# A hybrid transformer layer: its first norm as transposes, compression fed from PSUM, and another order of projections and attention

## The chip, the cores and the metric

The kernel runs on one core of a Trainium2 chip. A core has five engines that run side by side, each with its own queue of instructions in order: PE (TensorE: matmuls from SBUF into PSUM, which has 8 banks of 128 partitions by 512 fp32), DVE (VectorE), ACT (ScalarE), POOL (GpSimd, which sees SBUF only) and SP (SyncE, which issues DMAs). An instruction that waits holds up all that are behind it on its engine. The metric is the device time of one execution in microseconds: before the change 849.62 us, the median of 3 runs (848.8 to 850.38).

## The reference

One layer on x of 512 tokens by 1024, in fp32. Cut to what matters here:

```python
h = rms_norm(x, mix_norm_pre)
y = h @ w_in                      # q, kc vc, ksl vsl, kwn vwn, gates, mq mk mv, mi mf, mo
k_cmp = compress_blocks(kc, cmp_pos_k, w1_k, w2_k)   # blocks of 32 tokens, stride 16: 31 blocks
v_cmp = compress_blocks(vc, cmp_pos_v, w1_v, w2_v)   # silu((blocks + pos) @ w1) @ w2
o = gate0 * softmax(q k_cmp) v_cmp + gate1 * softmax(q ksl) vsl + gate2 * softmax(q kwn) vwn
mq, mk = silu(causal_depthwise_conv(mq, mk))         # width 4
y_ml = sigmoid(mo) * rms_norm(mlstm(mq, mk, mv, mi, mf))
x = x + rms_norm(concat(o, y_ml) @ w_out)
x = x + rms_norm(cross_attention(rms_norm(x), mem)); x = x + rms_norm(swiglu(rms_norm(x)))
```

There are 8 attention heads in 2 groups (kv 0 and 1) of width 64, and 4 mlstm heads. The 8 blocks of 64 tokens are all selected, so the selected branch is causal attention.

## The kernel before, in words

Matmuls of fp32 data run as three passes on a high and a low part (`split`: ACT makes `hi`, and VectorE or GpSimd makes `lo` = source - `hi`; `mm3` at L286 to L288: low x high, high x low, high x high). `H` holds the normed and turned x as such a pair, 1024 on partitions (8 k tiles) by 512 tokens.

**Head** (written out by hand, so its order on four engines is the order of the code). Rows of 128 tokens: `square_of` (ACT) sums squares, `gain_of` (VectorE, L480) multiplies x by the gain spread over partitions, `factor_of` takes the root (GpSimd) and makes a diagonal of it (L485), `turn_row` (L491) is eight fp32 matmuls of x by that diagonal, which the chip runs as 16, `parts_of` splits the result into `H` (`hTh`, `hTl`). `gates_and_v` is projection A of a row, 24 matmuls of 288 columns into `bk_A`: attention's values and all gates; its weights are split into `wah`, `wal` as they land. `bk_A` has PSUM tag "d" with two buffers; `keep_a` empties one: `vf`, `vr` and `gt_all`, `gl` (L512). Then come the mlstm's values `bk_mv`.

**Middle.** `PLAN["order"]` lists what is started in turn, and a scheduler with priorities orders the instructions on each engine by it. Lower-case names are projections, each name one tile: `c0`, `c1` convolution pairs, `m0`, `m2` the mlstm's output gate, `kc` the compression's input, `ks` keys, `q0` queries. Each tile splits 1024 x 128 weights (`whi`, `wlo`), runs 24 matmuls into `bk_dT` (tag "d") and has an evacuation: `ev_conv` (L709 to L716), `ev_mo` (L723, L724), `ev_kcvc`. The last adds the positions into `Xr` (L811, eight VectorE instructions of 64x248) and splits them into `Xb`. `Ck` and `Cv` are the compression's first matmul, 8 weight splits `w1s` and 16 matmuls into `bk_hb` (L880); each `Ck` in the list runs two of the eight. `S` and `O` are an mlstm head's scores (`bk_ms`, weighted into `sT`; L764 makes the weights from `rb`, a row fetched from DRAM to all partitions) and output (`bk_mn`, `hnat`, `ym`). `bk_ms`, `bk_hb` and attention's `bk_sc` and `bk_pc` share PSUM tag "sc" with three buffers.

**Attention.** `PLAN["units"]` lists 16 units (kv, row, pair of heads). Each runs `scores` (`bk_sc`, L977 to L981, `mx` is the minimum beside it) and then `values` of the unit before (transposes `bk_tr`, products `bk_pv`). `PLAN["fill"]` puts other work after a unit: `q` a query tile of kv 1, `C` the compressed branch of kv 0 (`compressed`: `bk_pc`, then on VectorE L682 to L695, and transposes `bk_pcT`), `m` and `k` of the memory. Then w_out, cross-attention and the feed-forward follow.

Of the kernel before, what the change touches and what calls it, by code (L numbers as in the profile page):

```python
# [86 lines left out]

# [1365 lines left out]
```

## Time and profile before

| | |
|---|---|
| median of 3 runs | 849.62 us (848.8 to 850.38) |
| the profiled execution | 849.66 us, of which its span is 847.9 |
| PE busy in the span | 821.3 us (97%) |
| DVE busy | 542.3 us (64%) |
| ACT busy | 425.1 us (50%) |
| POOL busy | 299.2 us (35%) |
| chain that ended last: PE | 78% |
| the same: DVE, ACT, POOL | 7%, 3%, 1% |

The profile is of one execution. Busy time is the time in which an engine ran an instruction, so TensorE's 821.3 us include those at a lower clock. The rows further down are from the trace of the same execution. "A <- B" in a list of waits says that A stood idle until B was done; a row's bracket at its end is the idle time before it. Times are us from the start of the span.

### The profile page before, as it was taken

The page shows a single profiled execution, that of the slowest core. Times are in us where ns is not written, and L with a number is a line of the kernel's source. Part 1 is how long each engine was busy: PE and PEld are TensorE (multiplying, and loading weights), DVE is VectorE, ACT ScalarE, POOL GpSimd, SP SyncE. Part 2 cuts the span into 40 slices and gives each one's busy share as a digit, 9 for nine tenths or more (in the row PEclk, how much of TensorE's full clock was granted, in tenths as well). Part 3 has the DMA queues.
Part 4 walks back from the last instruction along what each step waited for, and adds up shares of the span by engine and source line. Part 5 has one row for each costly group of instructions (what it writes and reads, how often), then busy time and mean ns, then how long its engine had stood idle before and what let it go on. Part 6 is the DMA issues. An engine that isn't in the chain of part 4 may idle for free.

```text
span 847.9 us, 12708 instructions
## 1 busy us (share of the span) xinstructions
PE 821.3 (97%) x4870; PEld 707.7 (83%) x4870; DVE 542.3 (64%) x934; ACT 425.1 (50%) x840; POOL 299.2 (35%) x224
## 2 busy tenths in 40 slices
PE   8999989999999999999999999999999999999997
PEld 5977767886688978778888889999999999888885
DVE  5738696697879835843453769988877885224323
ACT  5524565858867743743452556444444444324311
POOL 2043332355537542511320111444444444323320
PEclk9999999998999999999999999999999999999999
DMA  8371323221203232251341033333333322232102
GB/s 246 95 229 63 100 66 107 99 69 50 76 1 100 94 133 73 70 179 53 137 160 50 0 125 105 121 111 111 111 113 113 108 106 100 100 100 100 49 26 75
DMA packets 67763, 83.18 MB, mean 98 GB/s; under 512 B 4368, under 2 KB 53873, under 8 KB 67702
## 3 DMA queue, kind: packets, MB, share of 16 engines
q1 hardware_dynamic: 64574, 77.97, 28.3%
q10 hardware_dynamic: 3128, 4.40, 1.6%
q8 instruction: 38, 0.62, 0.3%
q14 instruction: 23, 0.19, 0.1%
HBM read 80.24 MB, written 2.12 MB: 97 GB/s over the span
## 4 chain that ended last, share of the span: by engine, by line
PE 78%; DVE 7%; ACT 3%; issue 1%; POOL 1%; DVEq 0%; ACTq 0%; POOLq 0%
PE bk_X L1301 5%; PE bk_X L1302 5%; PE bk_X L1303 5%; PE bk_ff L286 5%; PE bk_ff L288 5%; PE bk_ff L287 5%; PE bk_dT L286 4%; PE bk_dT L287 4%; PE bk_dT L288 4%; PE bk_pv L1027 3%; PE bk_dN L287 3%; PE bk_dN L286 3%; PE bk_dN L288 3%; PE bk_Z L1301 2%; PE bk_Z L1302 2%; PE bk_Z L1303 2%
## 5 line engine op out<-in xcount | busy, mean ns | idle before, releaser
L166 ACT ACTIVATE whi<-raw 128x1024 fp32r<-128x1024 f32 (+1 forms) x80 | 76.8, 968 | 63.4 <-PE bk_dT L286 27.8
L167 DVE TENSOR_TENSOR wlo<-raw,whi 128x1024 fp32r<-128x1024 f32 x41 | 54.2, 1323 | 81.5 <-PE bk_ff L287 43.0
L167 POOL TENSOR_TENSOR wlo<-raw,whi 128x1024 fp32r<-128x1024 f32 x23 | 55.8, 2428 | 106.4 <-ACT whi L166 104.6
L166 ACT ACTIVATE wh<-raw 128x1024 fp32r<-128x1024 f32 x64 | 67.3, 1057 | 49.3 <-PE bk_X L1301 16.1
L167 POOL TENSOR_TENSOR wl<-raw,wh 128x1024 fp32r<-128x1024 f32 x19 | 55.5, 2921 | 97.5 <-ACT wh L166 70.2
L286 PE MATMUL bk_dT<-hTh,wlo 128*128 128x512 f32 x192 | 76.9, 401 | 1.1 <-DVE wlo L167 0.8
L287 PE MATMUL bk_dT<-hTl,whi 128*128 128x512 f32 x192 | 76.3, 397 | 0.0
L288 PE MATMUL bk_dT<-hTh,whi 128*128 128x512 f32 x192 | 76.1, 396 | 0.0
L167 DVE TENSOR_TENSOR wl<-raw,wh 128x1024 fp32r<-128x1024 f32 x45 | 64.6, 1440 | 9.2 <-ACT wh L166 9.2
L167 POOL TENSOR_TENSOR gs<-gf,gs 128x512 fp32r<-128x512 f32 x22 | 32.4, 1478 | 65.9 <-ACT gs L166 65.9
L1302 PE MATMUL bk_X<-A,wh 128*128 128x256 f32 x192 | 54.5, 284 | 1.0 <-DVE A L167 1.0
L1301 PE MATMUL bk_X<-A,wl 128*128 128x256 f32 x192 | 54.4, 283 | 0.4 <-ACT A L166 0.4
L1303 PE MATMUL bk_X<-A,wh 128*128 128x256 f32 x192 | 54.3, 283 | 0.0
L287 PE MATMUL bk_ff<-wlo,gs 128*128 128x512 f32 x128 | 49.8, 389 | 0.0
L288 PE MATMUL bk_ff<-whi,gs 128*128 128x512 f32 x128 | 49.6, 389 | 0.0
L1301 PE MATMUL bk_X<-AS,wl 128*128 128x256 f32 x160 | 45.6, 285 | 2.4 <-ACT u L1356 2.3
L286 PE MATMUL bk_ff<-whi,gs 128*128 128x512 f32 x128 | 47.4, 389 | 0.0
L997 POOL TENSOR_SCALAR s<-s,acf 128x128 f32<-128x128 f32 (+3 forms) x32 | 36.5, 1151 | 26.7 <-PE bk_tr L1012 15.9
L1302 PE MATMUL bk_X<-AS,wh 128*128 128x256 f32 x160 | 44.9, 281 | 0.0
L1301 PE MATMUL bk_Z<-AS,wl 128*128 128x256 f32 x160 | 44.9, 281 | 0.0
L1303 PE MATMUL bk_X<-AS,wh 128*128 128x256 f32 x160 | 44.9, 281 | 0.0
L1303 PE MATMUL bk_Z<-AS,wh 128*128 128x256 f32 x160 | 44.9, 280 | 0.0
(376 smaller groups left out, 2535.2 us busy)
## 6 DMA issues: line engine op xcount, KB each, us to landing
raw<-in_w_gate_up_dram SPq DMA_DIRECT2D x22, 1024.0 KB, 6.5
raw<-in_w_down_dram SPq DMA_DIRECT2D x11, 1024.0 KB, 4.9
raw<-in_w_xkv_dram SPq DMA_DIRECT2D x8, 1024.0 KB, 5.1
raw<-in_w_in_dram SPq DMA_DIRECT2D x7, 1024.0 KB, 5.3
raw<-in_w_out_dram SPq DMA_DIRECT2D x4, 1024.0 KB, 5.1
raw<-in_w_xq_dram SPq DMA_DIRECT2D x4, 1024.0 KB, 5.4
raw<-in_w_xo_dram SPq DMA_DIRECT2D x4, 1024.0 KB, 5.1
raw<-in_w_in_dram SPq DMA_DIRECT2D x6, 512.0 KB, 4.7
```

Of the source, the lines that this page charges most:

```text
L166: first = nc.scalar.activation(hi, src, AF.Copy)
L167: second = (eng or nc.vector).tensor_tensor(lo, src, hi.bitcast(F32), op=OP.subtract)
L286: nc.tensor.matmul(o, lhsT=wl, rhs=xh, start=start, stop=False)
L287: nc.tensor.matmul(o, lhsT=wh, rhs=xl, start=False, stop=False)
L288: return nc.tensor.matmul(o, lhsT=wh, rhs=xh, start=False, stop=stop).ins
L997: ENG[on].tensor_scalar(s[:, 0:n], s[:, 0:n], c, None, op0=OP.mult)
L1027: nc.tensor.matmul(o, lhsT=v, rhs=pTs[br][q][:, j], start=(br, j, q) == mms[0], stop=(br, j, q) == mms[-1])
L1301: nc.tensor.matmul(o, lhsT=wl[:, k, c], rhs=A.hi(n, k), start=st, stop=False, skip_group_check=True)
L1302: nc.tensor.matmul(o, lhsT=wh[:, k, c], rhs=A.lo(n, k), start=False, stop=False, skip_group_check=True)
L1303: nc.tensor.matmul(o, lhsT=wh[:, k, c], rhs=A.hi(n, k), start=False, stop=stop and k == 3, skip_group_check=True)
```

## The change

The head makes the normed row on VectorE (`norm_half`: x times factor times gain) and turns it by transposes. Rows of x are fetched earlier, row 1's turn lies between the two halves of projection A of row 0, and `keep_a` of a row comes after the parts and the norm of later rows. The compression's input is copied to its hi part by ACT straight out of PSUM and the lo part is subtracted by VectorE (64x496 each); the positions go into a column (block 31) that no block uses, and `fold`, by which `bk_hb` is turned, adds that column to all blocks. The first step of the convolution and the output gate's scale go from VectorE to ACT. `rd` and `rb` go from ACT's DMA queue to SP's, `rb` two heads ahead. Half of v's weight splits come in halves, in other buffers. Two lists change.

```diff
-        "order": "c0 Lk c0 Lv kc m0 m0 Ck Ck Ck Ck c1 kc S0 O0 c1 "
-                 "S1 Cv Cv Cv Cv m2 S2 m2 O2 ks O1 ks q0 S3 q0 O3",
+        "order": "c0 Lk c0 Lv kc m0 Ck Ck m0 Ck Ck c1 kc S0 O0 c1 "
+                 "Cv S1 Cv m2 Cv S2 Cv m2 O2 ks O1 ks q0 S3 q0 O3",
-        "fill": ["C", "", "", "q", "q", "", "mk", "", "ck", "k", "kkk", "k", "k", "", "", ""],
+        "fill": ["q", "", "C", "q", "", "", "mk", "", "ck", "k", "kkk", "k", "k", "", "", ""],
-        "w1tv": "WWWWWWWW",
+        "w1tv": "GWGWGWGW",
...
-    def gain_of(i, g):
+    def factor_of(i):
+        factor[i] = rstd_of(factor[i], 1)
+
+    def norm_half(i, g):
         if g == 0:
-            xg[i] = x4([P, D], name="xg")
+            xn[i] = x4([P, D], name="xn")
         c = slice(512 * g, 512 * g + 512)
-        nc.vector.tensor_tensor(xg[i][:, c], res(i)[:, c], g_in[g], op=OP.mult)
-
-    def factor_of(i):
-        r = rstd_of(dg[i], 1)
-        dg[i] = small([P, P], "mt1")
-        nc.vector.tensor_scalar(dg[i], ident, r, None, op0=OP.mult)
+        nc.vector.scalar_tensor_tensor(xn[i][:, c], res(i)[:, c], factor[i], g_in[g], op0=OP.mult, op1=OP.mult)
...
-            nc.tensor.matmul(b[:, 128 * k:128 * k + 128], lhsT=xg[i][:, 128 * kk:128 * kk + 128], rhs=dg[i],
-                             start=True, stop=True)
+            nc.tensor.transpose(b[:, 128 * k:128 * k + 128], xn[i][:, 128 * kk:128 * kk + 128], ident)
...
             done = gates_and_v(i, 1)
-            last = (done, *keep_a(i - 1))
             if i + 2 < NT:
                 square_of(i + 2)
-                for g in range(2):
-                    gain_of(i + 2, g)
+                factor_of(i + 2)
             if then:
                 for g in range(2):
                     parts_of(i + 1, g)
+            if i + 2 < NT:
+                for g in range(2):
+                    norm_half(i + 2, g)
+            last = (done, *keep_a(i - 1))
...
-    nc.scalar.dma_start(rd, rr)
+    nc.sync.dma_start(rd, rr)
...
-            nc.vector.tensor_scalar(y, u, cw(c, 3), cb(c), op0=OP.mult, op1=OP.add)
+            nc.scalar.activation(y, b, AF.Identity, scale=cw(c, 3), bias=cb(c))
...
-            nc.vector.tensor_scalar(sg[c], sg[c], 1.0, hn(c), op0=OP.add, op1=OP.mult)
+            nc.scalar.activation(sg[c], sg[c], AF.Identity, scale=hn(c), bias=hn(c))
...
-                for q in range(2):
-                    nc.vector.tensor_tensor(Xr[q][64 * r:64 * r + 64, :, 32 * kv:32 * kv + 31],
-                                            full[:, r, :, q:q + 31],
-                                            pt[:, 8 * q:8 * q + 8].rearrange("p (j o) -> p j o", o=1).to_broadcast([64, 8, 31]),
-                                            op=OP.add)
...
-                split(B[:, :, 0, :], B[:, :, 1, :], X[:, 4 * g:4 * g + 4, :], engines("xb")[g])
...
+                full.append(bass.AP(tensor=one.tensor, offset=one.offset, ap=[one.ap[0], [16, 2], [2, 8], [16, 31]]))
+                to.append(X[64 * r:64 * r + 64, :, :, :, 32 * kv:32 * kv + 31])
+        for q in range(4):
+            nc.scalar.activation(to[q][:, :, :, 0], full[q], AF.Copy)
+        for q in range(4):
+            nc.vector.tensor_tensor(to[q][:, :, :, 1], full[q], to[q][:, :, :, 0].bitcast(F32), op=OP.subtract)
...
+    every = small([P, 1], "every", 1)
+    nc.vector.tensor_copy(every, fold[:, 31:32])
+    nc.vector.tensor_scalar(fold, fold, every, None, op0=OP.add)
```

The rows below are what stands in an engine's queue. VectorE in the head, from `hTl` of row 1 on, before (`vr` and `gl` are of `keep_a`; `xg` and `mt_275` the row times the gain and the diagonal):

```order
L167 TENSOR_TENSOR hTl<-bk_pn,hTh 128x4x128 x2
L232 TENSOR_SCALAR rs_e<-ss 128x1
L485 TENSOR_SCALAR mt_275<-cc,rs_r 128x128
L167 TENSOR_TENSOR vr<-bk_A,vr 128x2x64
L512 TENSOR_TENSOR gl<-bk_A,gb 128x8
L480 TENSOR_TENSOR xg<-xin,gain 128x512 x2
L167 TENSOR_TENSOR hTl<-bk_pn,hTh 128x4x128 x2
```

and now:

```order
L166 TENSOR_TENSOR hTl<-bk_pn,hTh 128x4x128 x2
L482 SCALAR_TENSOR_TENSOR xn<-xin,rs_r,gain 128x512 x2
L231 TENSOR_SCALAR rs_e<-ss 128x1
L166 TENSOR_TENSOR hTl<-bk_pn,hTh 128x4x128 x2
L482 SCALAR_TENSOR_TENSOR xn<-xin,rs_r,gain 128x512 x2
L166 TENSOR_TENSOR vr<-bk_A,vr 128x2x64
L508 TENSOR_TENSOR gl<-bk_A,gb 128x8
L166 TENSOR_TENSOR hTl<-bk_pn,hTh 128x4x128 x2
```

`vr` and `gl` of row 0 stood ahead of the gain step and the parts of row 2, and stand behind the parts of row 2 and the norm of row 3.

ACT around the first `Ck`, before (`qm`, `kmA` are of the mlstm's scores, `u` of the convolution):

```order
L709 ACTIVATE u<-bk_dT 128x512
L828 ACTIVATE qm<-zc 64x512
L715 ACTIVATE u<-zc 128x512
L166 ACTIVATE whi<-raw 128x1024
L824 ACTIVATE kmA<-zc 64x512 x2
L747 DMA rb<-rd 128x512
L166 ACTIVATE Xb<-Xr 128x4x64 x4
L764 ACTIVATE sT<-rb,ub 128x128 x3
```

and now:

```order
L715 ACTIVATE u<-bk_dT 128x512
L716 ACTIVATE zc<-bk_dT,chan 128x512
L831 ACTIVATE qm<-zc 64x512
L165 ACTIVATE w1s<-w_700 128x2x256
L721 ACTIVATE u<-zc 128x512
L821 ACTIVATE Xb<-bk_dT 64x16x31 x4
L165 ACTIVATE w1s<-w_702 128x2x256
L827 ACTIVATE kmA<-zc 64x512 x2
L165 ACTIVATE whi<-raw 128x1024
```

The convolution's first step has come in, the copies of `Xb` have nearly twice the elements per partition and come from `bk_dT`, and `whi` stands behind them.

VectorE at the first units of attention, before (`pc`, `mn`, `cf` are of the branch; `s,mx` of a unit's scores; `qst` of a query tile):

```order
L684 TENSOR_TENSOR pc<-pc,bk_pc 128x256
L687 TENSOR_REDUCE mn<-pc 128x16
L688 TENSOR_TENSOR pc<-pc,mn 128x512
L829 SCALAR_TENSOR_TENSOR qst<-bk_dT,qst 64x512
L691 TENSOR_REDUCE cf<-pc 128x16
L791 TENSOR_SCALAR hnat<-hnat,rs_r 128x128 x4
L829 SCALAR_TENSOR_TENSOR qst<-bk_dT,qst 64x512
L692 RECIPROCAL cf<-cf 128x16
L981 ISA s,mx<-bk_sc,nB 128x256
```

and now, some 20 instructions later in the queue:

```order
L690 TENSOR_TENSOR pc<-pc,bk_pc 128x256 x2
L693 TENSOR_REDUCE mn<-pc 128x16
L694 TENSOR_TENSOR pc<-pc,mn 128x512
L697 TENSOR_REDUCE cf<-pc 128x16
L698 RECIPROCAL cf<-cf 128x16
L699 TENSOR_TENSOR cf<-cf,gt_all 128x16
L700 TENSOR_SCALAR cf<-cf,cc 128x4
L701 TENSOR_TENSOR pc<-pc,cf 128x512
L993 ISA s,mx<-bk_sc,nB 128x128
```

The branch's steps stood between those of the last queries and of `hnat`; they stand in one piece, after `hnat` and the scores of the first units.

## Rows read from the trace of the kernel before

**Rows 1.** Windows: stretch; us, busy time per engine (instructions), clock, DMA share, GB/s.
```profile
10.00:36.00 26.00, 23.42 (x160) 21.27 (x159) 17.21 (x35) 14.53 (x38) 4.95 (x7) 1.00 0.39 127
80.00:110.00 30.00, 28.80 (x136) 22.74 (x136) 20.91 (x36) 15.80 (x34) 10.20 (x8) 1.00 0.41 113
110.00:130.00 20.00, 15.23 (x63) 10.79 (x62) 19.13 (x43) 15.78 (x42) 7.35 (x6) 0.91 0.08 20
180.00:200.00 20.00, 17.21 (x78) 13.22 (x76) 17.87 (x63) 11.77 (x29) 12.87 (x12) 0.83 0.20 59
```

**Rows 2.** The same view, two us inside the start of attention.
```profile
196.00:198.00 2.00, 2.00 (x9) 1.68 (x8) 1.68 (x6) 2.00 (x9) 1.57 (x2) 0.50 0.22 43
```

**Rows 3.** Waits of TensorE, 10 to 36 us: sum, times, longest.
```profile
PE bk_A L287 <- POOL wal L167: 1.4, 3, 0.8
PE bk_A L286 <- DVE hTl L167: 0.5, 1, 0.5
```

**Rows 4.** Waits of TensorE, 80 to 130 us.
```profile
PE bk_hb L880 <- DVE w1s L167: 2.9, 3, 1.6
PE bk_ms L756 <- DVE sT L766: 1.7, 1, 1.7
PE bk_dT L286 <- DVE wlo L167: 0.8, 2, 0.6
```

**Rows 5.** Waits of TensorE, 180 to 200 us.
```profile
PE bk_sc L977 <- DVE mx L981: 1.1, 1, 1.1
PE bk_mt L792 <- DVE hnat L791: 1.0, 1, 1.0
PE bk_pcT L698 <- DVE pc L695: 0.6, 1, 0.6
```

**Rows 6.** Timeline of TensorE, head: start, duration, instruction, count.
```profile
7.35 3.75 PE L491 MATMUL bk_pn<-mt,xg 128*128 128x128 f32 x16
...
18.46 1.95 PE L491 MATMUL bk_pn<-mt,xg 128*128 128x128 f32 x16
```

**Rows 7.** Timeline of TensorE, 227 to 230 us.
```profile
227.92 1.04 PE L254 MATMUL bk_pn<-cc,xn 128*128 128x128 f32 x8
```

**Rows 8.** Instructions of line 250: duration in ns, least, median, most.
```profile
L250 DVE SCALAR_TENSOR_TENSOR xn<-xin,rs_r,gain x12: 742/749/753, 335.6 to 497.3; 128x512 f32<-128x512 f32 x12
```

**Rows 9.** Timeline of VectorE, head.
```profile
13.19 1.89 DVE L480 TENSOR_TENSOR xg<-xin,gain 128x512 f32<-128x512 f32 x2
...
22.69 0.28 DVE L167 TENSOR_TENSOR vr<-bk_A,vr 128x128 fp32r<-128x128 f32 x1
23.23 0.17 DVE L512 TENSOR_TENSOR gl<-bk_A,gb 128x8 f32<-128x8 f32 x1 [0.26 <-ACT gt_all L511]
23.32 1.29 DVE L480 TENSOR_TENSOR xg<-xin,gain 128x512 f32<-128x512 f32 x2
24.76 0.69 DVE L167 TENSOR_TENSOR hTl<-bk_pn,hTh 128x512 fp32r<-128x512 f32 x1 [0.15 <-ACT hTh L166]
```

**Rows 10.** Groups of ACT, 60 to 150 us: count, busy us, mean ns, idle before.
```profile
L166 ACT ACTIVATE Xb<-Xr 128x256 fp32r<-128x256 f32 x8 | 2.7, 409 | 1.8 <-DVE Xr L811 1.8
...
L709 ACT ACTIVATE u<-bk_dT 128x512 f32<-128x512 f32 x4 | 2.3, 580 | 0.0
```

**Rows 11.** Windows, TensorE instructions of bk_dT alone, 97 to 103 us.
```profile
97.00:103.00 6.00, 6.00 (x28) 4.86 (x27) 0.00 (x0) 0.30 (x1) 1.00 0.60 177
```

**Rows 12.** Groups of VectorE, 80 to 130 us.
```profile
L811 DVE TENSOR_TENSOR Xr<-bk_dT,chan 64x248 f32<-64x248 f32 x16 | 6.0, 409 | 0.1
...
L710 DVE TENSOR_SCALAR zc<-u,chan 128x512 f32<-128x512 f32 x2 | 4.2, 2080 | 4.9 <-ACT u L709 4.9
L167 DVE TENSOR_TENSOR Xb<-Xr,Xb 128x256 fp32r<-128x256 f32 x8 | 4.0, 555 | 0.0
```

**Rows 13.** Groups of VectorE, 180 to 200 us.
```profile
L682 DVE TENSOR_TENSOR pc<-bk_pc,nB 128x7 f32<-128x7 f32 (+3 forms) x16 | 1.7, 166 | 0.0
...
L695 DVE TENSOR_TENSOR pc<-pc,cf 128x512 f32<-128x512 f32 x1 | 0.7, 693 | 0.0
```

More of the change, by code (lines that the diff above doesn't have):

```diff
@@ L531, in hybrid_layer @@
         nc.scalar.activation(g_in[1], spread[1], AF.Copy)
-        gain_of(0, 0)
+        square_of(1)
         factor_of(0)
-        turn_row(0, 0)
-        gain_of(0, 1)
-        turn_row(0, 1)
+        for g in range(2):
+            norm_half(0, g)
+            turn_row(0, g)
         warm_up(2)
-        parts_of(0, 0)
+        factor_of(1)
+        for g in range(2):
+            parts_of(0, g)
         split_a(0)
-        parts_of(0, 1)
+        norm_half(1, 0)
         split_a(1, 2, 3)
         raw_m = [load_m(0)]
+        norm_half(1, 1)
         gates_and_v(0, 0)
         for g in range(2):
-            gain_of(1, g)
+            turn_row(1, g)
+        square_of(2)
         split_a(4, 5)
-        square_of(1)
-        factor_of(1)
+        factor_of(2)
+        for g in range(2):
+            parts_of(1, g)
         split_a(6, 7)
@@ L551, in hybrid_layer @@
         gates_and_v(0, 1)
-        square_of(2)
         for g in range(2):
-            turn_row(1, g)
-        for g in range(2):
-            gain_of(2, g)
-        for g in range(2):
-            parts_of(1, g)
+            norm_half(2, g)
         for i in range(1, NT):
             then = i + 1 < NT
-            if then:
-                factor_of(i + 1)
             gates_and_v(i, 0)
@@ L575, in hybrid_layer @@
                     parts_of(i + 1, g)
+            if i + 2 < NT:
+                for g in range(2):
+                    norm_half(i + 2, g)
+            last = (done, *keep_a(i - 1))
     with ExitStack() as behind:
@@ L638, in hybrid_layer, with load_rb @@
     rd = dr.tile([4, 512], F32, name="rd")
-    nc.scalar.dma_start(rd, rr)
+    nc.sync.dma_start(rd, rr)
+    rbs = {}
+    def load_rb(h):
+        if h < 4:
+            rbs[h] = sgran(name="rb")
+            nc.sync.dma_start(rbs[h], rd[h:h + 1, :].to_broadcast([P, 512]))
+    for h in range(2):
+        load_rb(h)
     nc.vector.tensor_tensor(ir, ir, br_, op=OP.subtract)
@@ L767, in mlstm_scores @@
             sT.append(W[:, c0:c0 + n])
+        load_rb(h + 2)
         return sT
@@ L874, in comp @@
         for s in range(8):
-            take = x4 if PLAN["w1t" + n][s] == "T" else w4
-            w = take([P, 2, 2, 256], F32R, name="w1s")
-            split(w[:, :, 0, :], w[:, :, 1, :], w1r[n, s // 4][s % 4], engines("w1" + n)[s])
+            take = PLAN["w1t" + n][s]
+            if take == "G":
+                w = [gran((P, 2, 256), F32R, name="w1s") for _ in range(2)]
+                for k in range(2):
+                    split(w[k][:, 0, :], w[k][:, 1, :], w1r[n, s // 4][s % 4][:, k], engines("w1" + n)[s])
+            else:
+                t = (x4 if take == "T" else w4)([P, 2, 2, 256], F32R, name="w1s")
+                split(t[:, :, 0, :], t[:, :, 1, :], w1r[n, s // 4][s % 4], engines("w1" + n)[s])
+                w = [t[:, k] for k in range(2)]
             for k in range(2):
                 kk = 2 * s + k
-                nc.tensor.matmul(hb[n], lhsT=Xb[n][kk // 4][:, kk % 4].rearrange("p q b -> p (q b)"),
-                                 rhs=w[:, k].rearrange("p q c -> p (q c)"), start=kk == 0, stop=kk == 15)
+                nc.tensor.matmul(hb[n], lhsT=Xb[n][:, kk // 8, kk % 8].rearrange("p q b -> p (q b)"),
+                                 rhs=w[k].rearrange("p q c -> p (q c)"), start=kk == 0, stop=kk == 15)
             if s == 7:
```

28 lines of the change are left out of this document (11 added, 17 removed), and 1 row of the table PLAN.

## The prediction

> **What bounds the kernel now.** I read the table of engines first: TensorE is busy for 821.3 us of a span of 847.9, so the kernel is bound by TensorE and 26.6 us at most can be won without taking work off it. The view of busy time by stretch [rows 1] says where that idle time lies in the part that the diff touches. Of 10 to 36 us TensorE is busy 23.42 of 26.00 (2.6 idle), of 80 to 110 it is busy 28.80 of 30 (1.2), of 110 to 130 only 15.23 of 20 (4.8), of 180 to 200 it is 17.21 of 20 (2.8). [...] Work at half clock counts as busy but costs double: (1 - 0.91) x 20 = 1.8 us and (1 - 0.83) x 20 = 3.4 us. So the middle (80 to 130) loses 6.0 + 1.8 = 7.8 us, and the start of attention (180 to 200) 2.8 + 3.4 = 6.2 us.
>
> Then the waits of TensorE, stretch by stretch. In the head it waits for the low halves of the gate weights (`wal`) from GpSimd and once for `hTl` [rows 3]. In the middle 5.4 us of the 6.0 end with VectorE: 2.9 for the split compression weights `w1s`, 1.7 for `sT`, 0.8 for `wlo` [rows 4]. VectorE is busy there for 20.91 + 19.13 = 40.0 of 50 us, in the later part for 19.13 of 20 [rows 1]: it is a queue that is full, not one late instruction. At the start of attention again three waits, all for VectorE: `mx`, `hnat`, `pc` [rows 5].
>
> **The head.** Each row of x was turned by 16 fp32 matmul passes against a diagonal of the row's factor: 3.75 us for row 0 at the lower clock, 1.95 at the higher [rows 6]. It becomes 8 transposes; the same eight, elsewhere, take 1.04 [rows 7]. Three rows save 3 x (1.95 - 1.04) = 2.7, and row 0, half the passes at the same clock, 1.9: 4.6 together. Against it, on row 0's path `xn` (0.75 us a half [rows 8]) stands where a short diagonal stood: -0.7. Row 1's turn now lies between the halves of row 0's projection A, so the wait for `hTl` (0.5) should go and half of the 1.4 for `wal` be filled: +1.2 (bounds 0 and 1.9). A new wait comes in. Projection A has two PSUM buffers, and row 2 needs the one that `keep_a(0)` empties. Before, `vr` to `gl` (22.69 to 23.40, 0.7 us) ran ahead of the next row's gain steps [rows 9]; now they are queued on VectorE behind both `hTl` of a row and both `xn` of the next. After the turn of row 2 that is about 0.6 (the ACT half, sized as the PSUM copies of [rows 10]) + 0.7 + 1.5 + 0.7 + gaps of 0.2 = 3.7 us, while TensorE has 12 matmuls, some 1.6 us at 0.13 each (the 0.23 of [rows 11] scaled from 512 to 288 columns): 2.1 lost. For row 3 there are no more `xn`: 3.7 - 1.5 - 1.6 = 0.6. Together -2.7. Last, `xn` can collide with GpSimd: the gain steps took 1.89 a pair beside GpSimd's `wal` and 1.29 alone [rows 9], so -0.6 for one pair. Sum: 4.6 - 0.7 + 1.2 - 2.7 - 0.6 = **+1.8 us**. Bounds: -0.7 if nothing is filled and two pairs collide; +5.8 if the bank wait and the collisions do not come (4.6 - 0.7 + 1.9).
>
> [...]
>
> **The middle, VectorE.** Of its work in 80 to 130 us 16 position additions `Xr` (6.0), 8 `Xb` splits (4.0) and two first convolution steps (4.2) go [rows 12]: 14.2. Eight subtractions of 64x496 from PSUM come, which the trace lacks: not less than the 64x248 at 0.41 [rows 12], not more than a 128x512 `hTl` at 0.69 [rows 9]; nearer the second by elements, so 0.65 x 8 = 5.2. Net -9.0 of 40.0. That is larger than each wait it has to remove. ACT takes over eight copies of 64x496 out of PSUM (strided; 0.58 by the 128x512 copy, 4.6) and four full-width steps (2.3), and loses eight `Xb` at 0.41 (3.3) [rows 10]: +3.6 on 15.80 + 15.78 = 31.6 of 50 [rows 1]. GpSimd loses its memsets of `Xr`.
>
> **The middle, order.** The four steps of a compression were in one row, and their weights' splits came late by up to 1.6 us; now a projection tile stands between pairs. One tile is 24 matmuls at about 0.23 (28 touch a stretch of 6.00 us, two of them its edges) = 5.5 us [rows 11], in which eight halves at 0.6 can be made. The price is in front: one `m0` tile instead of two lies between the `kc` tile and the first Ck. ACT has four copies there (2.3) and about five other full-width instructions at 0.6 queued around them (3.0): 5.3 against 5.5, just hidden, but `whi` of the next `m0` waits behind them: 0 to 2.2, I take 1.2. Scores S2, now right after Cv's pair and S1, shares three PSUM buffers with the compression's accumulator: 0 to 1.2, I take 0.6. The clock falls once more behind what stalls remain: 1.0. So 7.8 - 2.8 = **+5.0**, bounds 0 and 7.8. `rd` and the `rb` loads move from ACT's queue to SP's, past raw weight loads that are wanted much later, and `rb` is fetched a score ahead: nothing on the path, as ACT's one visible wait for `rb` (outside these stretches) held nothing that TensorE waited for.
>
> **The start of attention.** The compressed branch is a chain on VectorE, from 16 small additions (1.7) to `pc` (0.7), with four more wide steps like the last and some small ones between: about 6 of the 17.87 us that VectorE is busy in 180 to 200 [rows 1, 13]. It now comes after unit 2, in one run, and a `q` tile stands at unit 0. `hnat` and the `mx` of the first units no longer queue behind it: 1.0 + 1.1 gone. `pc` and whatever waits behind the chain come later, and there TensorE has only scores and small transposes left, since the tile has been spent: 2.7 lost anew. Of the 6.2 I take **+3.5** (bounds +6.2 and -2.0, the latter if the chain's 6 us in one run leaves TensorE idle for 4 us more than now, less the 2 gone).
>
> Sum: 1.8 + 5.0 + 3.5 = 10.3. The profiled execution took 849.66 (span 847.9 and 1.8 around it), 0.04 above the median of 849.62, so no correction: 849.66 - 10.3 = **839.3 us**. After 245 us nothing changes.
>
> **Rivals.**
> - *All stalls go.* Head 5.8, middle 7.8, attention 6.2: 849.66 - 19.8 = 829.9. For it: nearly all waits name VectorE, which gets 9 us less. Against: two stalls that I derive are new.
> - *The branch's stall only moves.* Attention 0: 842.8. For it: the chain is as long as before, and in one piece. Against: `hnat` stood behind it and no longer does.
> - *ACT becomes the bound in the middle.* Its 3.6 us more, in front of `whi` and `w1s`, eat the 5.0; with attention 2.0: 849.66 - 3.8 = 845.9. Against: 31.6 of 50 busy.
> - *Slower: strided copies.* Four 64x496 copies per tile with a stride of 16 out of PSUM; the trace has no such access. If one takes 1.7 us instead of 0.58, each tile's four cost 4.5 more, with 0.2 of slack: two tiles 8.6 on the path, and nothing of the middle is won. 849.66 + 8.6 - 1.8 - 3.5 = 853.0. It decides from (1.8 + 3.5) / 8 + 0.58 = 1.25 us a copy. Against: the 64x248 additions with the same strides took 0.41, no more than their size explains [rows 12].
> - *Transposes leave the clock low.* Row 0's turn ran at the lower clock although warm-up matmuls precede it [rows 6]. If 8 transposes raise it later than 16 matmuls did, projection A of row 0 starts slow; the nearest price is what half clock cost that turn, 3.75 - 1.95 = 1.8: 841.1. [...]
>
> **How the numbers follow.** The forecast has 0.40 (its own range 835 to 844), all stalls gone 0.11, branch moved 0.18, ACT 0.14, strided copies 0.12, clock 0.05. The range leaves out the slower rival and a little at the other end: 830 to 849. About 0.2% (1.7 us) is what a measurement of this kernel can tell from no change. Faster by more: 0.40 + 0.11 + 0.18 + 0.05 and half of ACT's = 0.81; within: 0.06, the rest of ACT's nearly; slower: 0.13.
>
> **What would show it.** Head: turns of about 1.0 us and no `L491`-like pairs of passes; a wait of the first matmul of rows 2 and 3 for `gl` of about 2 and 0.6 us; the last `bk_A` some 2 us earlier. Middle: TensorE busy for at least 47.5 of the 50 us that answer to 80 to 130, VectorE below 35, no wait of `bk_hb` for `w1s` over 0.5; a 64x496 copy near 0.6 and a subtraction near 0.65. Attention: no wait for `hnat`, one for `pc` or `mx` at units 2 to 4 of up to 2.7. I am wrong if the copies are above 1.25 us, if TensorE's idle time up to 245 us is not smaller by 5 us or more, or if the clock falls in places where it did not before.

## The result and the profile after

The changed kernel took 856.4 us, the median of 4 runs (854.7 to 858.5), against 849.8 for the kernel before on the same chip: ratio 1.0087, 95% interval 1.0066 to 1.0108. Six more runs beside other kernels gave 857.3 against 849.0, again 1.0087 (1.0061 to 1.0113). It is slower by 0.9%, where 839.3 and a gain were forecast. The profiled execution is the slowest of the four, 858.5 with a span of 856.7; so it lies some 2 us above the median.

TensorE did have less to do: 817.5 us busy instead of 821.3, with 32 matmul passes fewer, those of the turns. It stood still for 39.2 us instead of 26.6. The stretches of [rows 1] in the changed kernel, and one more, since the branch has moved behind 200 us:

```profile
10.00:36.00 26.00, 21.64 (x121) 19.14 (x120) 15.78 (x29) 12.43 (x33) 5.33 (x6) 0.93 0.41 123
80.00:110.00 30.00, 26.54 (x117) 20.93 (x116) 16.63 (x26) 19.44 (x40) 8.44 (x6) 0.94 0.31 88
110.00:130.00 20.00, 16.35 (x75) 13.30 (x74) 17.10 (x33) 14.77 (x39) 7.89 (x8) 0.91 0.22 57
180.00:200.00 20.00, 18.85 (x109) 16.40 (x109) 17.67 (x61) 14.98 (x46) 14.15 (x13) 0.94 0.25 73
200.00:220.00 20.00, 15.84 (x70) 10.43 (x69) 15.34 (x64) 10.61 (x32) 7.11 (x8) 0.81 0.17 53
```

The line to look at is the pair of 80 to 130 us. VectorE (third engine column) is down from 40.0 to 33.7 us, as forecast (below 35), and TensorE is idle for 7.1 us there instead of 6.0. VectorE has less to do, and TensorE waits longer. In the head the granted clock is now 0.93, where it was 1.00.

The waits of TensorE behind these sums, in the stretches 10 to 36, 80 to 130 and 200 to 220 us (the lines that answer to [rows 3 to 5]):

```profile
PE bk_A L285 <- DVE gl L508: 2.7, 2, 2.0
PE bk_A L286 <- POOL wal L166: 1.0, 2, 0.5
...
PE bk_dT L285 <- DVE wlo L166: 4.2, 2, 3.7
PE bk_hb L892 <- ACT whi L165: 2.9, 1, 2.9
...
PE bk_pcT L704 <- DVE pc L701: 3.5, 1, 3.5
```

Of the waits of before, those for `hTl`, `w1s` and `hnat` are gone; `mx` is down from 1.1 to 0.3 us, `wal` from 1.4 to 1.0, and `sT` from 1.7 to 1.2 (it comes behind 130 us now). Four of 2.0 to 3.7 us have come up, for `gl`, `wlo`, in front of `bk_hb` and for `pc`, each longer than the longest of before (1.7). (In the second profile of the changed kernel, e8, `hnat` waits 1.3 and `pc` 2.5.)

**The new wait in the head** is the one that was worked out (2.1 and 0.6 us for rows 2 and 3). TensorE's first matmul of row 2, with VectorE's queue in front of it:

```profile
26.66 0.46 PE L285 MATMUL bk_A<-wah,hTl 128*128 128x288 f32 x1 [2.03 <-DVE gl L508]
...
33.20 0.37 PE L285 MATMUL bk_A<-wah,hTl 128*128 128x288 f32 x1 [0.70 <-DVE gl L508]
```

```profile
23.28 1.29 DVE L166 TENSOR_TENSOR hTl<-bk_pn,hTh 128x512 fp32r<-128x512 f32 x2 [2.66 <-ACT hTh L165]
24.48 1.41 DVE L482 SCALAR_TENSOR_TENSOR xn<-xin,rs_r,gain 128x512 f32<-128x512 f32 x2
25.81 0.28 DVE L166 TENSOR_TENSOR vr<-bk_A,vr 128x128 fp32r<-128x128 f32 x1
26.35 0.17 DVE L508 TENSOR_TENSOR gl<-bk_A,gb 128x8 f32<-128x8 f32 x1 [0.26 <-ACT gt_all L507]
```

`gl` ends at 26.52 behind both `hTl` and both `xn`, and the matmul that needs the PSUM buffer starts at 26.66. What the forecast did not price is the clock: in the windows behind this wait it is granted at 0.70, then 0.50, then 0.95.

```profile
26.00:28.00 2.00, 1.34 (x6) 1.37 (x7) 0.26 (x2) 0.19 (x1) 0.00 (x0) 0.70 0.04 8
28.00:30.00 2.00, 2.00 (x11) 1.98 (x10) 0.00 (x0) 0.00 (x0) 0.00 (x0) 0.50 0.00 0
30.00:32.00 2.00, 2.00 (x17) 2.00 (x17) 0.86 (x2) 1.42 (x4) 0.00 (x0) 0.95 0.00 0
```

**In front of the first Ck** the timeline of ACT shows what the 2.9 us are:

```profile
82.35 0.63 ACT L721 ACTIVATE u<-zc 128x512 f32<-128x512 f32 x1 [3.14 <-DVE zc L719]
82.88 2.34 ACT L821 ACTIVATE Xb<-bk_dT 64x496 fp32r<-64x496 f32 x4
85.25 0.63 ACT L165 ACTIVATE w1s<-w 128x512 fp32r<-128x512 f32 x1
```

ACT stood idle for 3.14 us, waiting for the convolution's `zc`, with the four copies of `Xb` queued behind that instruction. `zc` in turn was late on VectorE. Three convolution steps of nearly one size took 1.83 and 1.67 us where GpSimd was at work on a `wlo` and a `dg`, and 0.73 where it was not:

```profile
76.95 1.83 DVE L719 SCALAR_TENSOR_TENSOR zc<-u,chan,zc 128x509 f32<-128x509 f32 x1 [1.41 <-ACT zc L716]
...
79.53 1.67 DVE L719 SCALAR_TENSOR_TENSOR zc<-u,chan,zc 128x510 f32<-128x510 f32 x1
...
81.52 0.73 DVE L719 SCALAR_TENSOR_TENSOR zc<-u,chan,zc 128x511 f32<-128x511 f32 x1
```

```profile
75.85 2.38 POOL L166 TENSOR_TENSOR wlo<-raw,whi 128x1024 fp32r<-128x1024 f32 x1 [3.87 <-ACT whi L165]
...
78.90 1.75 POOL L754 TENSOR_TENSOR dg<-rb,cc 128x512 f32<-128x512 f32 x1
```

The same pattern comes back at 108 to 114 us (1.84 and 1.58 beside `wlo` and `dg`, then 0.75). Had the first two steps taken 0.73 as well, ACT would have come to the copies some 2.0 us earlier, an estimate from these rows, and most of the 2.9 would be gone.

VectorE's subtractions began only when all four copies had ended, and TensorE when they had:

```profile
85.26 2.73 DVE L823 TENSOR_TENSOR Xb<-bk_dT,Xb 64x496 fp32r<-64x496 f32 x4 [1.56 <-PE bk_dT L287]
```

```profile
84.87 0.39 PE L287 MATMUL bk_dT<-hTh,whi 128*128 128x512 f32 x1
88.13 1.11 PE L892 MATMUL bk_hb<-w1s,Xb 128*128 128x512 f32 x2 [2.88 <-ACT whi L165]
```

(The wait is put down to `whi`, which ended last; the matmul reads `Xb`, done at 87.99, and starts 0.14 us after it, as the one behind `gl` did after 26.52. The subtractions' idle time is put down to a matmul that ended at 85.26, 0.04 us after the copies; for the second `kc` tile the same idle time, 1.54, is put down to the copies.) Before, `Xb` was four tiles, each split by itself; now it is one. Whether that is why the four copies come as a block in front of the subtractions, no run tried. The durations were right: a copy took 0.578 us (0.58 forecast), a subtraction 0.672 (0.65).

**The longest wait, 3.65 us for `wlo`,** stands behind the same chain, at the second `kc` tile. The low part of the next projection's weights was queued on VectorE behind the four subtractions, which themselves waited for the copies; ACT was done with the high part at 121.94.

```profile
120.90 1.04 ACT L165 ACTIVATE whi<-raw 128x1024 fp32r<-128x1024 f32 x1
```

```profile
119.06 2.73 DVE L823 TENSOR_TENSOR Xb<-bk_dT,Xb 64x496 fp32r<-64x496 f32 x4 [1.54 <-ACT Xb L821]
...
123.60 1.22 DVE L166 TENSOR_TENSOR wlo<-raw,whi 128x1024 fp32r<-128x1024 f32 x1
```

```profile
124.87 0.50 PE L285 MATMUL bk_dT<-hTh,wlo 128*128 128x512 f32 x1 [3.65 <-DVE wlo L166]
```

### The profile page after: what moved, and what is told of

Its sections match the earlier page's. It is cut to its first block, busy times and chain, and to the rows that moved or that the text cites. A ratio compares the mean times of both kernels' runs of the same rounds, so it can differ in the third digit from the quotient of the medians.

```text
span 856.7 us, 12623 instructions
## 1 busy us (share of the span) xinstructions
PE 817.5 (95%) x4838; PEld 705.5 (82%) x4838; DVE 539.0 (63%) x911; ACT 433.4 (51%) x854; POOL 303.1 (35%) x225
## 4 chain that ended last, share of the span: by engine, by line
PE 76%; DVE 11%; ACT 6%; issue 3%; POOL 2%; DMA 1%; ACTq 0%; DVEq 0%; POOLq 0%; SPq 0%
PE bk_X L1313 5%; PE bk_ff L286 5%; PE bk_ff L285 5%; PE bk_ff L287 5%; PE bk_X L1314 5%; PE bk_X L1315 5%; PE bk_dT L285 4%; PE bk_dT L286 4%; PE bk_dT L287 4%; PE bk_dN L286 3%; PE bk_dN L285 3%; PE bk_dN L287 3%; PE bk_pv L1039 2%; PE bk_Z L1313 2%; PE bk_Z L1314 2%
## 5 line engine op out<-in xcount | busy, mean ns | idle before, releaser
L166 DVE TENSOR_TENSOR wl<-raw,wh 128x1024 fp32r<-128x1024 f32 x45 | 66.9, 1492 | 9.2 <-ACT wh L165 9.2
L285 PEld LDWEIGHTS bk_dT<-hTh,wlo 128*128 128x128 f32 x192 | 36.5, 190 | 14.5 <-DVE wlo L166 6.2
L1314 PE MATMUL bk_X<-AS,wh 128*128 128x256 f32 x160 | 44.4, 277 | 0.0
```

The costliest lines, as they stand in the source:

```text
L166: second = (eng or nc.vector).tensor_tensor(lo, src, hi.bitcast(F32), op=OP.subtract)
L285: nc.tensor.matmul(o, lhsT=wl, rhs=xh, start=start, stop=False)
L1314: nc.tensor.matmul(o, lhsT=wh[:, k, c], rhs=A.lo(n, k), start=False, stop=False, skip_group_check=True)
```

## The experiments

All times are medians; each kernel ran beside the kernel before, whose median lay between 849.0 and 850.1 from one comparison to the next. Executions of one kernel differ by up to 8.4 us (e4), so a difference of 1 us between two medians says little. A profile shows one execution.

**Undoing one thing of three.** Three runs undid, each alone, the late `keep_a`, the new list between units, and the new order.

```diff
             done = gates_and_v(i, 1)
+            last = (done, *keep_a(i - 1))
...
-            last = (done, *keep_a(i - 1))
```

> The changed kernel, with one line moved: keep_a(i - 1) directly after the second half of projection A of row i, ahead of the squares, parts and norm of later rows. Theory (the head's loss is the new wait for the PSUM buffer): the two waits for gl (2.0 and 0.7 us) go, and with the first the stretch at the lower clock behind it (12 matmuls of row 2 at 0.24 us instead of 0.13, 1.3 us): 856.4 - 4.0 = 852.4. Rival (the middle waits for something else in any case, and a later arrival of TensorE costs nothing there): 856.4, the waits gone all the same.

Measured 856.0 (ratio to before 1.0064, 1.0041 to 1.0087). The waits for `gl` are gone and projection A ends at 29.9 us instead of 36.3, yet the time is hardly better: the rival's number. TensorE then waits 6.4 us for `wlo` in the middle (4.6 in the changed kernel). The mean clock of its executions is 0.982 to 0.990, within the changed kernel's 0.982 to 0.993.

```diff
-        "fill": ["q", "", "C", "q", "", "", "mk", "", "ck", "k", "kkk", "k", "k", "", "", ""],
+        "fill": ["C", "", "", "q", "q", "", "mk", "", "ck", "k", "kkk", "k", "k", "", "", ""],
```

> The changed kernel with the old list of work between attention units (the branch at unit 0, the first query tile after unit 3). Theory (the branch in one run costs TensorE 3.5 us at unit 3, more than it did at unit 0): the loss between the first scores and w_out goes, about 3 us: 853.4. Rival (at unit 0 the branch stalls as much as in the kernel before, 2.8 us and a lower clock for 6.8 us): 856.4 or more.

Measured 855.1 (1.0054, 1.0037 to 1.0071), between the two. `pc` waits 0.2 us instead of 3.5, `mx` 2.5 instead of 0.3.

```diff
-        "order": "c0 Lk c0 Lv kc m0 Ck Ck m0 Ck Ck c1 kc S0 O0 c1 "
-                 "Cv S1 Cv m2 Cv S2 Cv m2 O2 ks O1 ks q0 S3 q0 O3",
+        "order": "c0 Lk c0 Lv kc m0 m0 Ck Ck Ck Ck c1 kc S0 O0 c1 "
+                 "S1 Cv Cv Cv Cv m2 S2 m2 O2 ks O1 ks q0 S3 q0 O3",
```

> The changed kernel with the old order of projections and compression steps (two m0 tiles, then four Ck; S1, then four Cv). Theory A (the order is what costs in the middle: one tile in front of the first Ck is too short for the chain ACT copies, VectorE subtractions): the wait of 2.9 us for Xb goes and the middle is won back, about 4 us: 852.4. Theory B (ACT's load is what costs, wherever the steps stand): no change within 1 us, 856.4.

Measured 856.2 (1.0071, 1.0050 to 1.0093), Theory B's number; in its profile the wait of 2.9 for `Xb` went and 3.8 for `w1s` from GpSimd came. (That execution took 851.8, of a range of 850.4 to 858.8.)

Against the changed kernel's median over all its ten runs, 857.1, these are 1.1, 2.0 and 0.9 us, 4.0 together. Undone one at a time nothing seemed to cost much. That is a reason to go from the other side.

**The head alone on the kernel before** (its first diff is the head's part of the change, with the order of the loads of x), first with the late `keep_a`, then with the early one (the diff of e1).

> The kernel before, with the new head alone (transposes, norm on VectorE, rows of x earlier, keep_a late). Theory: the last matmul of projection A comes 1.9 us later, as it does in the changed kernel, and all behind it moves by that: 849.8 + 1.9 = 851.7. Rival (the time lost in the head is given back at the waits of the middle, whose causes lie on other engines): 849.8. If the new head were a gain as predicted: 848.0.

Measured 847.1 (0.9970, 0.9956 to 0.9984): faster, against the theory of the moment and near the number of the prediction (848.0). The same two waits for `gl` are there, but the clock did not fall behind them in the profiled execution (1.00 in each window of 2 us from 26 to 34), and projection A ends at 33.9, only 0.5 us before the 34.4 of the kernel before.

```profile
25.80 0.37 PE L286 MATMUL bk_A<-wah,hTl 128*128 128x288 f32 x1 [2.02 <-DVE gl L509]
```

> The kernel before with the new head alone, and keep_a early. The new head with keep_a late gave 847.1 against 849.5. Theory (the two waits for gl, 2.7 us, were real idle time and nothing later waits for anything but TensorE's own work): 847.1 - 2.7 = 844.4, projection A ends near 30 us. Rival (VectorE and ACT are late in the middle anyway, so an earlier TensorE waits longer there): 847.

Measured 844.2 (0.9940, 0.9924 to 0.9957), as expected; it is the fastest of all, faster than both kernels, and of all the variants its six runs lie closest together (842.9 to 844.7). Projection A ends at 30.8.

**All three undone (the three diffs above together), and each put back alone.**

> The changed kernel with three things undone together: keep_a early, the old order of projections and compression, the old list between attention units. What is left of the change is the transposes, ACT's new work (Xb copies out of PSUM, first convolution step, gate scale), the half splits of v's weights and the rb queue. Each of the three alone left the median within 1.3 us of the changed kernel, but each took idle time away and the time at the lower clock grew. Theory (the idle times add up, and only when the last long wait is gone does the clock come back): about 848.3 - 4.7 - 3.7 - 3.4 = 836.5 without the clock's loss, and 843 with 6 to 7 us of it, faster than before. Rival (ACT's new work is what costs in the middle, whatever the order): 852 to 856.

Measured 845.9 (0.9966, 0.9945 to 0.9987): faster than before as expected, less than hoped; the rival is out.

> e5 (845.9: keep_a early, old order, old list) with the new list between attention units put back, alone. Theory (late keep_a, new order and new list each cost some 4.5 to 5.5 us, and two of them together, with 9.3 to 10.3 over e5, already nearly what all three cost): 845.9 + 5.6 = 851.5, of it 3.5 idle at the branch's pc and the rest at the lower clock behind it. Rival (only two of them together let the clock fall): 847 at most.

> e5 with the new order of projections and compression put back, alone. Theory: 845.9 + 4.6 = 850.5, with a wait of 2 to 3 us before the first matmuls of the compression and one of 3 to 4 us for wlo in front of the second c1 tile. Rival (the waits in the middle are as long in the old order, 3.4 for w1s and 3.1 for Xb, so the order changes nothing): 846.

> e5 with keep_a late again, alone. Theory: 2.7 us of waits for gl, and in executions in which the clock falls behind the first of them 2 us more: 845.9 + 2.9 (as on the kernel before) to + 4.8 = 848.8 to 850.7. Rival (the middle of e5 waits for other things anyway and swallows it): 846.

Measured 850.0, 850.6 and 849.3: the list costs 4.1 us over e5, the order 4.7, the late `keep_a` 3.4, near the theory each time. Together 12.2; the changed kernel stands 11.3 above e5 (857.1 over its ten runs). So from this side the medians do add up, while from the other side the same three came to 4.0. The waits that were expected are there: `pc` 3.8 us in e9 (1.3 in e5); `wlo` 3.7 at once and 2.6 before the first `bk_hb` in e10; `gl` 2.7 in e12. But only e9's stands alone. In e10 e5's waits of the middle, 3.4 for `w1s` and 3.1 for `Xb`, have gone, and TensorE is idle for 7.8 us of 36 to 130 where e5 has 8.2. What e10 has on top comes later: TensorE is idle for 2.4 us of 130 to 180 and 4.2 of 180 to 200, in e5 for 0.6 and 2.7. In e12's profile projection A ends 4.9 us later than in e5 and the first scores start 0.5 later: the middle waits less when TensorE comes later. Its span is only 0.2 longer than e5's, so this profile does not show how the 3.4 between the medians arises.

**The other edits of the middle.** Each is a part of e5; three runs took one back, three put one alone on e6.

```diff
-            nc.scalar.activation(y, b, AF.Identity, scale=cw(c, 3), bias=cb(c))
+            nc.vector.tensor_scalar(y, u, cw(c, 3), cb(c), op0=OP.mult, op1=OP.add)
```

```diff
-            nc.scalar.activation(sg[c], sg[c], AF.Identity, scale=hn(c), bias=hn(c))
+            nc.vector.tensor_scalar(sg[c], sg[c], 1.0, hn(c), op0=OP.add, op1=OP.mult)
```

> e5 (845.9) with the convolution's first step and the gate scale back on VectorE. Theory (ACT's longer queue, not VectorE's, is what makes e5 1.7 us slower than the new head alone, since evacuations of Xb stand behind it): 843, better than both. Rival (VectorE gets 4 us of work back and stalls beside GpSimd again): 847 to 850.

> The kernel before with the new head, keep_a early (844.2), and the convolution's first step and the gate scale on ACT, alone. Theory (VectorE's load does not set TensorE's waits in the middle, the order in the queues does, so taking 5 us from VectorE is not a gain by itself): 844 to 848. Rival (less work on VectorE in 110 to 130 us, where it is busy for 19 of 20, shortens the waits for w1s and sT): 842 or less.

(the same lines, the other way, on e6)

```diff
-    nc.sync.dma_start(rd, rr)
+    nc.scalar.dma_start(rd, rr)
...
-        rb = rbs[h]
+        rb = mgran(name="rb")
+        nc.scalar.dma_start(rb, rd[h:h + 1, :].to_broadcast([P, 512]))
...
-        load_rb(h + 2)
```

> e5 with rd and rb back on ACT's DMA queue, fetched where they are used. Theory (the early rb on SP's queue hides a wait of 0.6 to 1.8 us on ACT and GpSimd that TensorE does not see): 846 +- 1. Rival (with ACT's fuller queue rb is now on the path): 849.

> The kernel before with the new head, keep_a early (844.2), and rd and rb on SP's queue, rb two heads ahead, alone. Theory (ACT's wait of 1.8 us for rb near 133 us held nothing that TensorE needed): 844.2 +- 1. Rival (the score weights come earlier and the wait of 1.7 us for sT goes): 842.

(again the other way) For the evacuation of `kc` the edit is `ev_kcvc` as a whole, with `fold`'s three lines, back in e11 and new in f3.

> e5 with the old evacuation of the kc tiles (position additions of 64x248 on VectorE, then the splits). What is left of the change: transposes, convolution's first step and gate scale on ACT, half splits, the rb queue. Theory (the chain of four ACT copies and then four VectorE subtractions holds the PSUM buffer of the projections and TensorE waits 3.1 us for it): that wait goes, 845.9 - 3 = 843, no later than the new head alone (844.2). Rival (VectorE is full again with 16 additions and 8 splits, 9 us more): 849.

> The kernel before with the new head, keep_a early (844.2) and the new evacuation of the kc tiles alone. Taking the old evacuation back in e5 cost 8.5 us, but by another order of the engines' queues (a new wait of 5.8 us before bk_mn). Theory (16 additions and 8 splits less are worth something in the VectorE-bound stretch of 110 to 130 us): 841 to 843. Rival (copies and then subtractions, one after the other, hold the projections' PSUM buffer, wait of 3 us): 846.

| edit | taken back in e5 (845.9) | alone on e6 (844.2) |
|---|---|---|
| convolution step, gate scale on ACT | f1 854.0 (+8.1) | g1 848.8 (+4.6) |
| rd, rb on SP's queue | f2 849.8 (+3.9) | g2 852.9 (+8.7) |
| Xb copied from PSUM | e11 854.4 (+8.5) | f3 849.8 (+5.6) |

Every theory failed here, g1's by the least (848.8, where 844 to 848 was expected; its rival, 842, is out), and in both directions at once: each edit costs 4.6 to 8.7 us when it is put in, and 3.9 to 8.5 when it is taken out, though, with the half splits, all of them together cost 1.7 (the intervals of e5 and e6 overlap). (The kernel before stood at 849.0 beside e5 and e6 and at 849.2 to 850.1 beside the others, so a difference in the table can be off by 1 us.) No fixed price of an instruction does that.

g2 shows how it can come about. It changes only how `rd` and `rb` are fetched (the queue, the moment, and the buffers that `rb` takes), and of the 930 instructions of VectorE some 60 stand at another place in its order. VectorE's queue before v's compression, in e6:

```
L808 TENSOR_TENSOR Xr<-bk_dT,chan 64x8x31
L713 SCALAR_TENSOR_TENSOR zc<-u,zc 128x512
L167 TENSOR_TENSOR w1s<-w_748,w1s 128x2x256
...
L167 TENSOR_TENSOR Xb<-Xr,Xb 128x4x64 x4
L763 TENSOR_TENSOR sT<-sT,bk_ms 128x512
```

and in g2:

```
L818 TENSOR_TENSOR Xr<-bk_dT,chan 64x8x31
L723 SCALAR_TENSOR_TENSOR zc<-u,zc 128x512
...
L772 TENSOR_TENSOR sT<-sT,bk_ms 128x512
L772 TENSOR_TENSOR sT<-sT,bk_ms 128x384
...
L167 TENSOR_TENSOR w1s<-w_752,w1s 128x2x256
...
L167 TENSOR_TENSOR Xb<-Xr,Xb 128x4x64 x4
```

With `rb` there earlier, the scores' multiplications are put in front of the compression's splits, and TensorE waits for those, in g2 3.4 us at once, where e6 has 1.6 at most. This is read from the queues and was not tried by itself; the four `Xb` splits also took 2.51 us in g2 and 1.42 in e6.

```profile
PE bk_hb L887 <- DVE w1s L167: 4.5, 2, 3.4
```

```profile
PE bk_hb L877 <- DVE w1s L167: 3.4, 4, 1.6
```

```diff
-        "w1tv": "GWGWGWGW",
+        "w1tv": "WWWWWWWW",
```

> As e5, with v's compression weights split whole again (one 128x512 instruction instead of two of 128x256 for half of the steps). With the old order the first matmuls of the compression waited 3.8 us for GpSimd's split of w1s, 2.8 of it at once, and two 128x256 halves took 2.78 us on GpSimd where a whole one takes 1.3 to 1.5. Theory (the halves double GpSimd's work): e5 - 3 = 840. [...]

Measured 848.6 (0.9990, 0.9975 to 1.0005): the halves are a gain of 2.7, against the theory; the wait of 2.8 for GpSimd's split went, but waits for `hnat` (1.5) and VectorE's `w1s` (2.6) came.

**The clock.**

> The changed kernel itself, beside the others on one chip, for its spread: its four executions lay between 854.7 and 858.5 and their mean granted clocks between 0.986 and 0.993. If the clock is what separates them, time less (1 - clock) x span is the same in all within about 1.5 us, near 848.3; if not, the two do not go together.

Measured 857.3 (852.2 to 859.1). The fastest of the six had a mean clock of 0.992, the slowest 0.982; (1 - 0.992) x 850.4 = 6.8 and (1 - 0.982) x 857.3 = 15.4, so the clock makes 8.6 us where 6.9 lie between them. Less that loss the six lie between 841.6 and 845.4 and the first four between 846.5 and 849.5. So the expectation failed: the spread falls from 6.9 to 3.8 among the six and from 3.8 to 3.0 among the four, not to 1.5, and some 4 us are left between the two groups. The mean clock accounts for a part of what separates executions; the rest I can't explain.

```diff
             done = gates_and_v(i, 1)
+            b = bank("pv", "bk_warm") if then else None
+            for _ in range({1: 14, 2: 4}.get(i, 0)):
+                nc.tensor.matmul(b[:, 0:288], lhsT=H.hi(0, 0, 128), rhs=wa[0][0], start=True, stop=True)
```

> e12 (late keep_a in e5, 849.3) with 14 and 4 extra matmuls of 288 columns, whose result nobody reads, queued on TensorE in front of rows 2 and 3 of projection A, where it waits 2.0 and 0.7 us for gl. They take 0.13 us each, 1.85 and 0.5, so they end before gl comes. Theory (the lower clock behind the wait comes from TensorE standing still, and costs about 2 us more than the wait): row 2 runs at the full clock, projection A ends at 33.9 and not 36.1, 849.3 - 2 = 847.3. Rival (the clock falls for another reason, such as the transposes, or the late keep_a costs its waits alone): 849.3 or more.

Measured 851.9 (1.0029, 1.0013 to 1.0046), slower than e12: the theory failed. In the head row 2 ran at 0.13 us a matmul, and projection A ended at 33.9, not 36.1:

```profile
23.69 2.01 PE L564 MATMUL bk_warm<-wah,hTh 128*128 128x288 f32 x14
25.87 0.37 PE L285 MATMUL bk_A<-wah,hTl 128*128 128x288 f32 x1 [0.18 <-DVE gl L508]
```

But that is not the filler's doing. In the profile of e12 row 2 runs at 0.13 us too, behind a wait of 2.03 us that nothing fills; what e12 lost against f4 lies ahead of that wait, in row 1, where 12 matmuls from 19.8 us on ran at half pace, 0.24 us each:

```profile
20.00:22.00 2.00, 2.00 (x9) 2.00 (x10) 0.40 (x2) 0.00 (x0) 0.56 (x1) 0.50 0.42 77
...
28.00:30.00 2.00, 2.00 (x16) 2.00 (x17) 0.00 (x0) 0.00 (x0) 0.00 (x0) 1.00 0.03 8
```

So these two profiles do not show whether matmuls in the wait keep the clock up. Nor did the earlier end of the head last: the first scores start at 175.4 us in f4 and at 173.2 in e12. TensorE's wait for `Xb` is 3.1 in f4 instead of 1.5, as in e5 (3.1), whose projection A ends at 31.2.

## Why the prediction was wrong

The profiles give each stretch its share. The last matmul of projection A and the first scores of attention, in the kernel before and in the changed one (all instructions of a line; least, median, most in ns; first and last start in us):

```profile
L288 PE MATMUL bk_A<-wah,hTh x32: 292/294/357, 12.2 to 34.4; 128*128 128x288 f32 x32
L977 PE MATMUL bk_sc<-kA,qst x64: 278/376/688, 172.3 to 289.1; 128*128 128x256 f32 x32, 128*128 128x384 f32 x16, 128*128 128x512 f32 x16
```

```profile
L287 PE MATMUL bk_A<-wah,hTh x32: 292/294/442, 12.5 to 36.3; 128*128 128x288 f32 x32
L989 PE MATMUL bk_sc<-kA,qst x64: 274/384/664, 179.1 to 297.6; 128*128 128x256 f32 x32, 128*128 128x384 f32 x16, 128*128 128x512 f32 x16
```

| profiled execution | last matmul of projection A starts | first scores start | span |
|---|---|---|---|
| before | 34.4 | 172.3 | 847.9 |
| changed | 36.3 | 179.1 | 856.7 |
| changed again (e8) | 36.0 | 178.8 | 855.9 |
| e2: head, late `keep_a` | 33.9 | 171.9 | 845.0 |
| e6: head, early `keep_a` | 30.8 | 169.1 | 842.1 |
| e5: all three undone | 31.2 | 172.7 | 846.5 |
| e12: e5, late `keep_a` | 36.1 | 173.2 | 846.7 |

So the changed kernel has lost 1.9 us by the end of the head, 4.9 more by the first scores and 2.0 behind them, 8.8 in all, where +1.8, +5.0 and +3.5 were forecast.

**Head (+1.8; -1.9 in the changed kernel).** By itself the new head gained 2.3 (849.5 to 847.1), near the forecast, but by luck: in e2's profile it has gained 0.5 by the end of projection A, not 2, and 2.5 of the 2.9 us of its span arise behind the first scores. There TensorE is busy for 18.18 us at a clock of 0.91, before for 17.21 at 0.83 [rows 1]:

```profile
180.00:200.00 20.00, 18.18 (x91) 13.91 (x91) 18.84 (x71) 13.36 (x34) 13.69 (x12) 0.91 0.21 69
```

The turns (1.04 us at the full clock) and the waits for `gl` (2.03 and 0.70) are as forecast. What the sum lacks is matmuls at half pace, 0.24 us instead of 0.13, at two places: behind the wait for `gl`, 12 matmuls of row 2 in the changed kernel's profile, and at the start of row 0, which I had as a rival at 1.8 us (below). The -2.7 for the late `keep_a` comes from the order, not from the transposes: in e6 these waits are gone. The lower bound of the head's sum was added up wrongly: its own terms give 4.6 - 0.7 - 2.7 - 1.2 = 0.0, not -0.7. The collision of `xn` with GpSimd was sized too small: beside a `wal` split a pair took 2.31 us and one half 1.29, alone a pair takes 1.41 to 1.42, so 0.9 and 0.55, 1.45 in all and not 0.6, and not all on the path, since these rows of x are not needed at once.

```profile
18.25 2.31 DVE L482 SCALAR_TENSOR_TENSOR xn<-xin,rs_r,gain 128x512 f32<-128x512 f32 x2
```

```profile
18.00 2.01 POOL L166 TENSOR_TENSOR wal<-raw,wah 128x288 fp32r<-128x288 f32 x2 [1.69 <-ACT wah L165]
```

That is more than the row that I used, 0.3 a half: the pair lost 0.45 a half, the single one 0.55.

**Middle (+5.0, measured -4.9): the step that failed is "it is a queue that is full, not one late instruction".** I took 9 us of work from VectorE and credited TensorE with most of its idle time of before. VectorE did get lighter, by 6.3 us, and TensorE's idle time in 80 to 130 us rose from 6.0 to 7.1. The runs showed that the load did not set the waits: e5 has VectorE at 35.8 us in 80 to 130 and TensorE idle for 7.05, e6 at 39.5 and 7.02. g1 and f3, which take work off VectorE by one edit each, are slower than e6 as well.

```profile
80.00:130.00 50.00, 42.95 (x188) 33.89 (x187) 35.77 (x64) 36.85 (x85) 17.84 (x17) 0.93 0.25 70
```

```profile
80.00:130.00 50.00, 42.98 (x194) 32.79 (x193) 39.52 (x76) 30.22 (x72) 17.09 (x15) 1.00 0.30 79
```

In the changed kernel's profile the long waits come from the chain through two in-order queues and where a step stands in them. "5.3 against 5.5, just hidden" assumed that ACT starts on the copies as the `kc` tile ends; it stood 3.14 us behind a `u` that VectorE was late for, and copies and subtractions, 2.34 and 2.73, ran one after the other; they made the 2.9 in front of `bk_hb`. "`whi` of the next `m0` waits behind them", which I took at 1.2, was the right kind of term on the wrong engine: `wlo` stood behind the subtractions on VectorE, 3.65 us. And VectorE's busy time was no measure of its work: the two first convolution steps that I counted at 4.2 us [rows 12] took 2.08 on average, where the shortest in that kernel took 0.54. By the medians the order costs 4.7 (e10) and the other edits 1.7 together (e5 against e6), 6.4 in all. GpSimd, ACT and VectorE could each be late in turn. The 1.0 for the clock behind the stalls that remain was an estimate that no row gives; the mean clock in 80 to 130 us was 0.97 before and is 0.93 in the changed kernel.

**Attention (+3.5, measured -2.0 in the profile, -4.1 by e9).** Both halves of the step were seen: `hnat` and `mx` hardly wait, `pc` does, 3.5 us (2.7 forecast). The error is in their balance: that the clock would come back (3.4) was my estimate, which no row showed. The stretch of 180 to 200 us has 0.94 and that of 200 to 220 has 0.81, so the clock costs 1.2 + 3.8 = 5.0 us there instead of 3.4.

Summed by the runs: +2.3 - 6.4 - 4.1 = -8.2; measured -6.5 in the first runs and -8.3 in the second. That it fits is in part luck, since the single edits cost something else when they are undone from the changed kernel. What the runs show firmly is the sum of the three: 11.3 us for late `keep_a`, order and list together (e5), more than the whole loss.

**The rivals.** The change was slower for none of the reasons given. The strided copies took 0.58 us, not 1.25. ACT is busy for 34.2 of 50 us, so it is no bound, but it was late at one place. The branch's stall did move, and grew, from 0.6 to 3.5. The rival of the clock: in the profiled execution of the changed kernel row 0 ran at half pace until 16.7 us (0.24 us a matmul), where the kernel before was at full pace (0.13) from 13.2 on. Of the 19 profiles with the new head 16 have a stretch at half pace there, and the turn of row 1 takes 1.18 to 1.91 us; e1, f1 and f3, with the same eight transposes in front, have none behind the first matmul, and there it takes 1.03 or 1.04. So the slow start that the rival named did come, mostly. It is not what made the change slower: e2 and e6 have it too (1.21 and 1.30) and are faster than before. Whether the transposes are its cause was not tried. Nor do the rows show the slow start as a lower granted clock, as the prediction called it: from 6 to 18 us that clock is 1.00 in every window of 2 us in both kernels, though row 0's turn took 3.75 us in 16 passes [rows 6] and 1.94 in 8, later ones 1.95 and 1.04; in e3 it is 0.50 in 14 to 16 us.

**What stays open:** why the three edits of the table go together and not alone, for each pair of them; only g2 was followed to the rows. Why undoing one of the three big edits gains 0.9 to 2.0 us, and putting one back costs 3.4 to 4.7. Whether a version with Xb, convolution and rb can beat e6 was not found.

## What to carry to other kernels

When a list scheduler sets the order in the queues, an edit can cost far more than its instructions, by the order that comes out; so add edits one by one to the kernel before, and keep what gains (here one of them, 844.2), rather than undo them one by one from the sum, which showed little. That an engine is busy nearly all the time (here VectorE, 19.13 of 20 us) does not make its load the bound of a stretch; ask for the latency of the chain that the bound engine waits for, step by step, what stands in front of each step in its queue, and whether a step is slow while another engine runs beside it (here 1.83 us against 0.73). A wait can be followed by more loss than its length: behind one of 2.0 us the clock fell to 0.50 in three profiles of six here, and in the changed kernel's 12 matmuls then took 0.24 us instead of 0.13; look at the granted clock there in more than one execution before you put a price on it.
